# One tile in place of two for the decays of a state-space scan, with six buffers in place of four and two

## The chip, the cores and the metric

The kernel runs on one core of one Trainium2 chip. Its metric is the device time of one execution in microseconds (us), taken as the median of several runs. The core's engines are TensorE (PE, matrix products), VectorE (DVE), ScalarE (ACT), GpSimd (POOL) and SyncE (SP, which here issues nearly all DMA transfers). Each engine runs its own list of instructions strictly in order, and semaphores make one engine wait for another.

## The reference, cut to what matters

The program is one inference step of two layers, a gated pooling mixer and a gated Mamba-2 mixer (SSD), for 1024 prompt tokens and 64 sample tokens. The change touches the chunked scan of the second layer:

```python
a_cum_t = jnp.moveaxis(jnp.cumsum(a, axis=2), 2, -1)        # per chunk of 128 tokens, per head
causal = jnp.tril(jnp.ones((q, q), bool))
seg = a_cum_t[..., :, None] - a_cum_t[..., None, :]
L = jnp.exp(jnp.where(causal, seg, -jnp.inf))               # the decays
CB = jnp.einsum('bcign,bcjgn->bcgij', C, B)
W = CB[:, :, :, None] * L * dt_t[..., None, :]
y_diag = jnp.einsum('bcgeij,bcjgep->bcigep', W, x)
```

For each chunk of 128 tokens and each head a 128x128 matrix of decays L is formed, weighted with the products of C and B, and multiplied by the chunk's inputs.

## The kernel before

The tokens are worked in two halves, h=0 and h=1, of 512 prompt tokens and 32 sample tokens (544 columns). Activations lie with channels on the 128 partitions and tokens along the columns. The large projections (`product`, L172) split a weight tile of 128x1024 into a high and a low part (`whi`, `wlo`) and an activation likewise (`ah`, `al`); each 128x272 result takes 24 matmuls into one of three PSUM buffers called `big`, which an engine then copies or adds out: L184 into `u` on ACT, L761 and L762 into `z` on ACT and DVE, L790 and L791 into `X` on ACT and DVE. A PSUM buffer is free again only after this.

`stash` (L131 to L144) runs in the first half of the program, before about 650 us: it loads pieces of 128x512 of later weights, casts them (L141), subtracts (L142) and writes the low parts to DRAM, from where `wlo` is loaded later.

The scan (`ssd`, from L617) is called per half h, group g of heads and quad q of four heads, 16 calls in all, each with two pairs of chunks. For each chunk it loads the running sums of the decays, broadcast to all partitions (L632, a DMA on SP's queue, tile `bA`), masks them (L633, POOL), exponentiates them into a second tile `L` (L637, ACT, four instructions, one per head) and multiplies them by the chunk's weights `bs` (L638, DVE). For each pair of chunks PE then multiplies by the decays (L651, 16 matmuls into `dg`), reads the state (L665, `of` from `hf`) and forms the new states (L667, `stt`); POOL scales the old state (L672) and DVE adds the new one (L673). The sample tokens go the same way in `ssd_sample`: state tiles are loaded (L734), multiplied (L735), the new state is formed (L739), scaled on POOL (L741), added on DVE (L742) and stored (L743).

`ssd_common` (L598 to L603) makes, for a group, four transposes and four products on PE (L598, L599) and copies them to SBUF on ACT (L601 to `bs`, L603 to `bt`). At the end of a half, L858 (DVE) and L860 (POOL) scale the eight tiles `X` and add the residual.

The order of the instructions on each engine is not written by hand: the Tile framework's scheduler (L1028) decides it with its own model of time, from the program, the priorities (`tc.high_priority()` around PSUM copies and weight loads) and the number of buffers of each tile name. A tile name with `bufs=n` gives the n-th next tile the same memory, so that its first writer waits for the last reader of the tile n before it.

Of the kernel before, what the change touches and what calls it, by code (L numbers as in the profile page):

```python
# [9 lines left out]
F32 = mybir.dt.float32  # L10
F32R = mybir.dt.float32r
AF = mybir.ActivationFunctionType
ALU = mybir.AluOpType
# [3 lines left out]
P = 128  # L17
# [20 lines left out]
Q = 128  # L38
# [38 lines left out]
def pool_ssd_step(ctx, tc, xin, spool, sconv, sssm, w_pin, w_mix, w_pout, w_sin, w_dt, w_sout, params, consts,  # L77
                  y_out, pool_p, pool_s, conv_p, conv_s, ssm_p, ssm_s):
    nc = tc.nc
    V, S, G, PE = nc.vector, nc.scalar, nc.gpsimd, nc.tensor  # L80
# [4 lines left out]
    sp = ctx.enter_context(tc.tile_pool(name="sp", bufs=1))  # L85
# [45 lines left out]
    def stash(n):  # L131

        for k, src, a, b in todo[:n]:
            raw = sp.tile([P, 512], F32, name="L", bufs=4)[:, :b - a]
            load = nc.sync.dma_start(out=raw, in_=src[:, a:b])
            if behind[0] is not None:
                tc.add_manual_dep(load.ins, behind[0].ins.name,
                                  mybir.DependencyInfo(mybir.DependencyClass.NoSync, mybir.DependencyReason.DATA),
                                  reason="low parts come in behind the weights in use")
            hl = sp.tile([P, 512], F32R, name="bA", bufs=2)[:, :b - a]  # L140
            S.copy(hl, raw)  # L141
            V.tensor_tensor(out=hl, in0=raw, in1=hl, op=ALU.subtract)  # L142
            nc.sync.dma_start(out=low[k][:, a:b], in_=hl.bitcast(F32))
        del todo[:n]  # L144
# [139 lines left out]
    def project(src, act, u, evac):  # L284
        hi, lo = unit(src[u], k=LOW_IN + u if src is w_sin else None)
        stash(1)
        product(P, hi, lo, act, KT, P, 0, evac)
# [16 lines left out]
    def out_units(src, g, y, sink):  # L304
        for dpair in range(4):
            w = unit(src[g * 4 + dpair], k=LOW_OUT + g * 4 + dpair if src is w_sout else None)
            stash(1)
            out_unit(w, dpair, y, sink)


    def layer0(h, act, pending, nxt):
# [99 lines left out]
        def mix_part(g, p, z):  # L411
            tiles = []
            for mp in range(2):
                hi, lo = unit(w_mix[g * 2 + mp])
                stash(2 if h == 0 else 1)
                for tt in range(2):
                    t = mp * 2 + tt
                    y = z[t]

                    def gate(n, ps):  # L420
                        V.scalar_tensor_tensor(out=half(y, n), in0=ps, scalar=pcol(V_SC + g * 4 + t),
                                               in1=half(z[t], n), op0=ALU.mult, op1=ALU.mult)
                    product(P, hi, lo, p, 4, 256, tt * P, gate)
                    tiles.append(split(y, "y", t))
            return tiles
# [43 lines left out]
    acd = [dp.tile([NCH, NH, Q], F32, name=f"acd{h}") for h in range(2)]  # L469
# [137 lines left out]
    def heads(x):  # L607
        return x.rearrange("p (e d) -> p e d", e=4)
# [4 lines left out]
    def by_head(x, i):  # L613

        return x[:, i:i + 4, None].broadcast_to([x.shape[0], 4, HD])

    def ssd(h, g, q, x, ys, C, com, nat, cdb):  # L617
        h0 = g * 8 + q * 4
        hf = None
        if h == 1:  # L620
            hf = sp.tile([P, 2 * P], F32, name=f"hf{q}", bufs=2)
            nc.sync.dma_start(out=hf, in_=hsd[g, q])
        for c0 in range(0, NCH, 2):

            pd = sps.tile([P, 2, 2 * Q], F32, name="dg")
            xds, xss, Ls = [], [], []
            for c in (c0, c0 + 1):
                cs = slice(c * Q, (c + 1) * Q)
                ci = c * NH + h0

                bA = sp.tile([P, 4, Q], F32, name="bA", bufs=2)
                nc.sync.dma_start(out=bA, in_=acd[h][c:c + 1, h0:h0 + 4].broadcast_to([P, 4, Q]))  # L632
                G.affine_select(out=bA, in_=bA, pattern=[[0, 4], [1, Q]], compare_op=ALU.is_ge, fill=-1e30, base=0,  # L633
                                channel_multiplier=-1)
                L = sp.tile([P, 4, Q], F32, name="L", bufs=4)
                for e in range(4):
                    S.activation(out=L[:, e], in_=bA[:, e], func=AF.Exp, bias=nat[:, 0, ci + e:ci + e + 1])  # L637
                V.tensor_tensor(out=L, in0=L, in1=com[c][0].broadcast_to([P, 4, Q]), op=ALU.mult)  # L638
                px = sps.tile([P, 2 * P], F32, name="tr", bufs=2)
                for k in range(2):  # L640
                    PE.transpose(px[:, k * P:(k + 1) * P], x[:, k, cs], ident)  # L641
                xd = sp.tile([P, 2 * P], F32, name="xd", bufs=2)
                xs = sp.tile([P, 2 * P], F32, name="xs", bufs=2)
                for k, x1 in enumerate((xd, xs)):
                    V.tensor_tensor(out=heads(x1), in0=heads(px), in1=by_head(nat[:, 1 + k], ci), op=ALU.mult)
                xds.append(xd)
                xss.append(xs)
                Ls.append(L)
            for n in range(2):
                for e in range(4):  # L650
                    PE.matmul(pd[e % 2 * HD:(e % 2 + 1) * HD, e // 2, n * Q:(n + 1) * Q], xds[n][:, e * HD:(e + 1) * HD],  # L651
                              Ls[n][:, e], start=True, stop=True)
            first = 1 if hf is None else 0
            po = sps.tile([P, 2, 2 * Q], F32, name="of")
            bE = sp.tile([P, 2, 2 * Q], F32, name="bE")
            for n in range(2):
                c = c0 + n
                cs = slice(c * Q, (c + 1) * Q)
                ns = slice(n * Q, (n + 1) * Q)
                if hf is not None:  # L660
                    ev = ecd[h][c:c + 1, h0:h0 + 4].rearrange("c (k r) i -> c r k i", r=2)
                    for r in range(2):
                        nc.sync.dma_start(out=bE[r * 64:(r + 1) * 64, :, ns], in_=ev[:, r].broadcast_to([64, 2, Q]))
                    for k in range(2):
                        PE.matmul(po[:, k, ns], hf[:, k * P:(k + 1) * P], C[:, cs], start=True, stop=True)  # L665
                pst = sps.tile([P, 2 * P], F32, name="stt")
                PE.matmul(pst, com[c][1], xss[n], start=True, stop=True)  # L667
                hn = sp.tile([P, 2 * P], F32, name=f"hf{q}", bufs=2)
                if hf is None:
                    S.copy(hn, pst)  # L670
                else:
                    G.tensor_tensor(out=heads(hn), in0=heads(hf), in1=by_head(cdb, c * NH + h0), op=ALU.mult)  # L672
                    V.tensor_tensor(out=hn, in0=hn, in1=pst, op=ALU.add)  # L673
                hf = hn
            if first:
                S.copy(ys[:, :, c0 * Q:(c0 + 1) * Q], pd[:, :, :Q])
            fs = slice((c0 + first) * Q, (c0 + 2) * Q)
            V.tensor_tensor(out=ys[:, :, fs], in0=po[:, :, first * Q:], in1=bE[:, :, first * Q:], op=ALU.mult)
            V.tensor_tensor(out=ys[:, :, fs], in0=ys[:, :, fs], in1=pd[:, :, first * Q:], op=ALU.add)
        nc.sync.dma_start(out=ssm_p[g, q] if h == 1 else hsd[g, q], in_=hf)  # L680
# [99 lines left out]
    def layer1(h, act, started, pending, nxt):  # L780
# [26 lines left out]
        for g in range(NG):  # L807
# [6 lines left out]
            def quad(q):  # L814
                y = sp.tile([P, 2, T], F32, name="ys", bufs=2)
                ssd(h, g, q, xbc[2 * q], y, C, com, nat, cdb)
                ssd_sample(h, g, q, xbc[2 * q], y, C, scom, sat, cdb)
                return y
# [213 lines left out]
```

## Time and profile before

| what | value |
|---|---|
| runs (3), device time | 1584.18, 1584.54, 1586.19 us; median 1584.54 |
| the profiled execution | 1586.41 us, of which 1584.6 us are the profile's span |
| mean granted clock of TensorE in it | 0.995 of full speed |
| busy: PE, DVE, ACT, POOL | 98%, 68%, 46%, 21% of the span |
| chain of work that ended last | PE 87%, DMA 5%, DVE 4%, ACT 2% |
| share of L172's matmuls in that chain | 77% |

PE is busy nearly all of the time, so a change shows in the time where PE stands still or runs at a lower clock, and the other engines' idle time matters only where PE waits for them. The views used are the list of PE's waits, the views of one tile or line (its durations, first and last start, and what it waited for), the time line of one engine, the chain of waits, and tables of busy time by stretch.

### The profile page before, as it was taken

To read this page: it belongs to the slowest core of one execution; us is meant where nothing else is said; L and a number is where in the kernel's file an instruction comes from. 1 tells how busy PE (TensorE), PEld (TensorE's weight loads), DVE (VectorE), ACT (ScalarE), POOL (GpSimd) and SP (SyncE) were. 2 spreads that over 40 slices of the span, in tenths; PEclk is the share of its full clock that TensorE was granted. 3 is DMA by queue.
4 is the path that set the end of the run, shared out by engine and by line. 5 is a ranking of instruction groups with operands and counts; after the bars stand their busy time and mean duration, and the time that the engine had idled before them with its cause. 6 is when DMAs were issued, how large, how long until landed. Compare 5 with 4: busy or idle time off the path is not lost.

```text
span 1584.6 us, 33029 instructions
## 1 busy us (share of the span) xinstructions
PE 1554.3 (98%) x12644; PEld 1510.4 (95%) x12644; DVE 1085.3 (68%) x2068; ACT 734.0 (46%) x1454; POOL 333.9 (21%) x536
## 2 busy tenths in 40 slices
PE   9999999999999999999999999999998999999996
PEld 8999999999999999999999999999998999999995
DVE  7787778865557576658666476678778865755767
ACT  5553434544343434355565453543635645535432
POOL 1300000012100011013513112212326532231213
PEclk9999999999999999999999999999999999999998
DMA  7756656758555565565756656656666666565662
GB/s 258 245 191 186 206 167 218 252 183 274 185 172 188 168 195 187 165 197 154 244 183 200 201 173 218 209 190 219 206 206 210 215 217 205 176 218 176 210 218 86
DMA packets 163405, 315.80 MB, mean 199 GB/s; under 512 B 33072, under 2 KB 71600, under 8 KB 163248
## 3 DMA queue, kind: packets, MB, share of 16 engines
q1 hardware_dynamic: 163248, 313.70, 61.6%
q8 instruction: 99, 1.62, 0.4%
q14 instruction: 58, 0.48, 0.1%
HBM read 262.47 MB, written 51.16 MB: 198 GB/s over the span
## 4 chain that ended last, share of the span: by engine, by line
PE 87%; DMA 5%; DVE 4%; ACT 2%; issue 1%; POOL 1%; SPq 1%; DVEq 0%; POOLq 0%; ACTq 0%
PE big L172 77%; PE dg L651 2%; PE stt L667 2%; PE of L665 2%; DMA sq<-in_xin_dram 1%; PE tr L641 1%; DMA X<-in_xin_dram 1%; DVE X L858 1%; DMA L<-in_w_sin_dram 1%; PE stt L739 1%; PE big L392 1%; DMA out_ssm_s_dram<-ho 1%; PE of L735 1%; PE tr L599 0%; POOL ssq L251 0%
## 5 line engine op out<-in xcount | busy, mean ns | idle before, releaser
L172 PE MATMUL big<-ah,whi 128*128 128x272 f32 (+1 forms) x2304 | 668.5, 290 | 0.3 <-DVE X L428 0.3
L172 PE MATMUL big<-al,whi 128*128 128x272 f32 (+1 forms) x2304 | 668.6, 290 | 0.0
L172 PE MATMUL big<-ah,wlo 128*128 128x272 f32 (+1 forms) x2304 | 665.0, 289 | 0.0
L172 PEld LDWEIGHTS big<-ah,whi 128*128 128x128 f32 (+1 forms) x2304 | 432.7, 188 | 3.9 <-issue 2.3
L172 PEld LDWEIGHTS big<-ah,wlo 128*128 128x128 f32 (+1 forms) x2304 | 433.0, 188 | 2.8 <-issue 1.8
L172 PEld LDWEIGHTS big<-al,whi 128*128 128x128 f32 (+1 forms) x2304 | 432.8, 188 | 1.4 <-issue 0.4
L172 PE MATMUL big<-y,whi 128*128 128x272 f32 x2048 | 400.6, 292 | 4.7 <-DVE X L791 2.5
L155 ACT CAST whi<-raw 128x1024 fp32r<-128x1024 f32 (+1 forms) x228 | 237.6, 1042 | 334.2 <-PE big L172 248.2
L172 PEld LDWEIGHTS big<-y,whi 128*128 128x128 f32 x2048 | 322.9, 188 | 9.5 <-issue 3.1
L172 PE MATMUL big<-y,wlo 128*128 128x272 f32 x1024 | 298.3, 291 | 0.0
L157 DVE TENSOR_TENSOR wlo<-raw,whi 128x1024 fp32r<-128x1024 f32 x112 | 140.4, 1254 | 89.4 <-ACT whi L155 87.2
L172 PEld LDWEIGHTS big<-y,wlo 128*128 128x128 f32 x1024 | 193.5, 189 | 1.6 <-issue 1.0
L571 DVE SCALAR_TENSOR_TENSOR win<-u,par,win 128x556 f32<-128x556 f32 x144 | 119.4, 830 | 34.0 <-ACT win L569 31.6
L142 DVE TENSOR_TENSOR bA<-L,bA 128x512 fp32r<-128x512 f32 (+1 forms) x113 | 78.2, 693 | 31.3 <-ACT bA L141 27.9
L141 ACT CAST bA<-L 128x512 fp32r<-128x512 f32 (+1 forms) x113 | 69.9, 619 | 59.5 <-DMA L<-in_w_sin_dram 33.7
L172 PE MATMUL big<-p,whi 128*128 128x272 f32 x512 | 96.7, 288 | 0.0
L637 ACT ACTIVATE L<-bA,nat 128x128 f32<-128x128 f32 x256 | 80.2, 391 | 33.4 <-PE dg L651 24.8
L741 POOL TENSOR_TENSOR ho<-hs,cdb 128x256 f32<-128x256 f32 x64 | 47.2, 741 | 176.9 <-DMA out_ssm_s_dram<-ho 133.8
L172 PEld LDWEIGHTS big<-p,whi 128*128 128x128 f32 x512 | 80.3, 188 | 0.0
L331 POOL COPY uc<-u 128x15 f32<-128x15 f32 x30 | 22.2, 739 | 259.5 <-ACT u L184 169.2
L428 DVE TENSOR_TENSOR X<-X,big 128x272 f32<-128x272 f32 x128 | 54.3, 430 | 30.2 <-PE big L172 29.9
L184 ACT COPY u<-big 128x272 f32<-128x272 f32 (+2 forms) x192 | 52.5, 308 | 47.8 <-PE big L172 35.2
(212 smaller groups left out, 1964.7 us busy)
## 6 DMA issues: line engine op xcount, KB each, us to landing
wlo<-low SPq DMA_DIRECT2D x114, 512.0 KB, 3.9
raw<-in_w_sin_dram SPq DMA_DIRECT2D x80, 512.0 KB, 4.8
raw<-in_w_pin_dram SPq DMA_DIRECT2D x64, 512.0 KB, 3.9
low<-bA SPq DMA_DIRECT2D x112, 256.0 KB, 4.2
L<-in_w_sin_dram SPq DMA_DIRECT2D x80, 256.0 KB, 4.3
raw<-in_w_sout_dram SPq DMA_DIRECT2D x34, 512.0 KB, 4.7
raw<-in_w_pout_dram SPq DMA_DIRECT2D x32, 512.0 KB, 3.8
bA<-acd SPq DMA_DIRECT2D x64, 256.0 KB, 3.9
```

The source lines that it names most:

```text
L141: S.copy(hl, raw)
L142: V.tensor_tensor(out=hl, in0=raw, in1=hl, op=ALU.subtract)
L155: S.copy(hi[:, :cols], raw[:, :cols])
L157: V.tensor_tensor(out=lo[:, :cols], in0=raw[:, :cols], in1=hi[:, :cols], op=ALU.subtract)
L172: PE.matmul(ps, w[:, wsl], x[:, cols], start=first, stop=kt == kts - 1 and a == 2)
L184: S.copy(out, ps)
L428: return lambda n, ps: V.tensor_tensor(out=half(X[d], n), in0=half(X[d], n), in1=ps, op=ALU.add)
L571: V.scalar_tensor_tensor(out=a[:, :n], in0=x[:, k:k + n], scalar=pcol(V_CW + ti * 4 + k), in1=a[:, :n], op0=ALU.mult, op1=ALU.add)
L637: S.activation(out=L[:, e], in_=bA[:, e], func=AF.Exp, bias=nat[:, 0, ci + e:ci + e + 1])
L651: PE.matmul(pd[e % 2 * HD:(e % 2 + 1) * HD, e // 2, n * Q:(n + 1) * Q], xds[n][:, e * HD:(e + 1) * HD], Ls[n][:, e], start=True, stop=True)
L665: PE.matmul(po[:, k, ns], hf[:, k * P:(k + 1) * P], C[:, cs], start=True, stop=True)
L741: G.tensor_tensor(out=heads(ho), in0=heads(hs), in1=by_head(cdb, (NCH + b) * NH + h0), op=ALU.mult)
```

## The change

`bA` as a tile name of its own disappears. In `ssd` the decays are loaded into a tile `L`, masked in it and exponentiated in it, in place; `L` has six buffers where `L` had four and `bA` two, so that the memory taken is the same (2 KB a partition each). In `stash` the tile `hl` moves from `bA` to `L`. Each engine issues as many instructions as before. In the changed file every line from L636 on has a number lower by one.

```diff
     def stash(n):
...
-            raw = sp.tile([P, 512], F32, name="L", bufs=4)[:, :b - a]
+            raw = sp.tile([P, 512], F32, name="L", bufs=6)[:, :b - a]
...
-            hl = sp.tile([P, 512], F32R, name="bA", bufs=2)[:, :b - a]
+            hl = sp.tile([P, 512], F32R, name="L", bufs=6)[:, :b - a]
...
     def ssd(h, g, q, x, ys, C, com, nat, cdb):
...
-                bA = sp.tile([P, 4, Q], F32, name="bA", bufs=2)
-                nc.sync.dma_start(out=bA, in_=acd[h][c:c + 1, h0:h0 + 4].broadcast_to([P, 4, Q]))
-                G.affine_select(out=bA, in_=bA, pattern=[[0, 4], [1, Q]], compare_op=ALU.is_ge, fill=-1e30, base=0,
+                L = sp.tile([P, 4, Q], F32, name="L", bufs=6)
+                nc.sync.dma_start(out=L, in_=acd[h][c:c + 1, h0:h0 + 4].broadcast_to([P, 4, Q]))
+                G.affine_select(out=L, in_=L, pattern=[[0, 4], [1, Q]], compare_op=ALU.is_ge, fill=-1e30, base=0,
                                 channel_multiplier=-1)
-                L = sp.tile([P, 4, Q], F32, name="L", bufs=4)
                 for e in range(4):
-                    S.activation(out=L[:, e], in_=bA[:, e], func=AF.Exp, bias=nat[:, 0, ci + e:ci + e + 1])
+                    S.activation(out=L[:, e], in_=L[:, e], func=AF.Exp, bias=nat[:, 0, ci + e:ci + e + 1])
```

The scheduler places the work of the scan anew. Three places of the program follow, one of them on two engines; the numbers behind the names are the tiles.

SP at the opening of the scan (h=0, around 700 us before), from the loads of the first chunk pair on. First the order before:

```order
L632 DMA bA_8874<-acd0_143 128x512
L543 DMA esd0_151<-d2_8502 32x32
L663 DMA bE_8901<-ecd0_145 64x2x128 x2
L705 DMA bAs_8986<-asd0_149 32x128
L159 DMA wlo_9137<-low19_105 128x1024
L752 DMA bEs_9053<-esd0_151 64x2x32
L152 DMA raw_9469<-in_w_sin_dram 128x1024
L752 DMA bEs_9053<-esd0_151 64x2x32
L632 DMA bA_8919<-acd0_143 128x512
L632 DMA bA_8937<-acd0_143 128x512
```

And the order of the change in the same place:

```order
L632 DMA L_8873<-acd0_143 128x512
L543 DMA esd0_151<-d2_8502 32x32
L662 DMA bE_8899<-ecd0_145 64x2x128 x2
L632 DMA L_8917<-acd0_143 128x512
L159 DMA wlo_9133<-low19_105 128x1024
L632 DMA L_8934<-acd0_143 128x512
L152 DMA raw_9461<-in_w_sin_dram 128x1024
L704 DMA bAs_8982<-asd0_149 32x128
L751 DMA bEs_9049<-esd0_151 64x2x32 x2
L632 DMA L_9201<-acd0_143 128x512
```

The loads of the second pair (`bA_8919` and `bA_8937`, now `L_8917` and `L_8934`) have moved up past two weight loads and three loads for the samples; the third pair's follow where the second's were.

ACT in the same place, before:

```order
L569 ACTIVATE win0_8729<-u_8665,par_76 128x556
L184 COPY u_8738<-big_8747 128x272
L709 ACTIVATE bAs_8986<-bAs_8986 32x128
L155 CAST whi_9410<-raw_9408 128x1024
L184 COPY u_8738<-big_8773 128x240
L184 COPY u_8738<-big_8773 128x4x8
L637 ACTIVATE L_8924<-bA_8919,nat_8495 128x128 x3
L601 COPY bs_8813<-tr_8810 128x128
L603 COPY bt_8815<-tr_8810 128x128
L637 ACTIVATE L_8924<-bA_8919,nat_8495 128x128
L601 COPY bs_8820<-tr_8817 128x128
L603 COPY bt_8822<-tr_8817 128x128
```

And in the change:

```order
L569 ACTIVATE win0_8729<-u_8665,par_76 128x556
L636 ACTIVATE L_8917<-L_8917,nat_8495 128x128 x4
L184 COPY u_8738<-big_8747 128x272
L636 ACTIVATE L_8934<-L_8934,nat_8495 128x128 x4
L155 CAST whi_9402<-raw_9400 128x1024
L184 COPY u_8738<-big_8773 128x240
L184 COPY u_8738<-big_8773 128x4x8
L601 COPY bs_8813<-tr_8810 128x128
L603 COPY bt_8815<-tr_8810 128x128
L601 COPY bs_8820<-tr_8817 128x128
L603 COPY bt_8822<-tr_8817 128x128
```

The second pair's eight exponentials have moved ahead of three PSUM copies and a weight cast, and no exponential stands directly ahead of or between the copies L601 and L603 any more.

DVE at the end of the first half (around 1202 us before), where the eight L858 stand; before:

```order
L679 TENSOR_TENSOR ys<-ys,dg 128x2x256
L235 COPY rr<-tr 128x272 x2
L858 TENSOR_TENSOR X_10997<-X_10997,rr 128x544
...
L858 TENSOR_TENSOR X_11218<-X_11218,rr 128x544
L742 TENSOR_TENSOR ho<-ho,stt 128x256
L762 SCALAR_TENSOR_TENSOR z_15808<-z_15808,big 128x272
L754 TENSOR_TENSOR ys<-of,bEs 128x2x32
```

And in the change:

```order
L678 TENSOR_TENSOR ys<-ys,dg 128x2x256
L235 COPY rr<-tr 128x272
...
L741 TENSOR_TENSOR ho<-ho,stt 128x256
L857 TENSOR_TENSOR X_10981<-X_10981,rr 128x544
...
L857 TENSOR_TENSOR X_11202<-X_11202,rr 128x544
L753 TENSOR_TENSOR ys<-of,bEs 128x2x32
L761 SCALAR_TENSOR_TENSOR z_15768<-z_15768,big 128x272
```

The addition L742 of the first sample state (L741 in the changed file) has moved ahead of the eight scalings; the evacuation L762 of a `big` buffer (now L761) still stands behind them.

ACT in the first group of the second half (around 1293 us before), where copies L790 stand behind exponentials; before:

```order
L790 COPY X3_17066<-big_17067 128x272
L802 ACTIVATE sq_17225<-p2_16144 128x544
L637 ACTIVATE L_17720<-bA_17715,nat_14370 128x128 x4
L709 ACTIVATE bAs_16773<-bAs_16773 32x128
L637 ACTIVATE L_17738<-bA_17733,nat_14370 128x128 x4
L802 ACTIVATE sq_17233<-p2_16144 128x544
L155 CAST whi_17242<-raw_17240 128x1024
L790 COPY X3_17066<-big_17081 128x272
```

And in the change:

```order
L801 ACTIVATE sq_17177<-p2_16104 128x544
L801 ACTIVATE sq_17185<-p2_16104 128x544
L789 COPY X3_17018<-big_17019 128x272
L155 CAST whi_17194<-raw_17192 128x1024
L789 COPY X3_17018<-big_17033 128x272
L636 ACTIVATE L_17732<-L_17732,nat_14338 128x128 x4
L789 COPY X4_17053<-big_17054 128x272
L636 ACTIVATE L_17749<-L_17749,nat_14338 128x128 x4
```

The second copy of `X3` stood behind eight exponentials, two squares and a cast; now only the cast stands between the two copies of `X3`, and the exponentials follow them.

## Rows read from the trace of the kernel before

**Rows 1.** The page, part 1: busy time of each engine

```profile
PE 1554.3 (98%) x12644; PEld 1510.4 (95%) x12644; DVE 1085.3 (68%) x2068; ACT 734.0 (46%) x1454; POOL 333.9 (21%) x536
```

**Rows 2.** PE's waits: instruction <- its releaser: us in total, times, longest

```profile
PE stt L739 <- DVE ho L742: 4.1, 1, 4.1
...
PE tr L598 <- ACT bt L603: 1.9, 1, 1.9
...
PE of L665 <- DVE hf L673: 1.2, 1, 1.2
PE big L172 <- ACT X L790: 1.0, 1, 1.0
```

**Rows 3.** Tile `L`: ns min/median/max, first and last start us

```profile
L651 PE MATMUL dg<-L,xd x512: 272/273/324, 726.8 to 1516.5; 128*64 128x128 f32 x171
...
L638 DVE TENSOR_TENSOR L<-L,bs x64: 670/684/1168, 710.9 to 1486.1; 128x512 f32<-128x512 f32 x64
```

**Rows 4.** Tile `bA`: one line's durations, idle time by releaser, landing

```profile
L633 POOL TENSOR_SCALAR_AFFINE_SELECT bA<-bA x64: 627/635/1631, 698.8 to 1478.8; 128x512 f32<-128x512 f32 x64
...
  DMA bA<-acd: 114.8, 51
...
  PE dg L651: 24.8, 14
...
DMA to landing us min/median/max: 2.0/4.1/7.3
```

**Rows 5.** Time line of SP: start us, us, instruction

```profile
697.29 1.32 SPq L663 DMA_DIRECT2D bE<-ecd  x2
...
702.81 1.01 SPq L632 DMA_DIRECT2D bA<-acd  x2
...
728.87 1.76 SPq L632 DMA_DIRECT2D bA<-acd  x2
```

**Rows 6.** Chain of waits, 702 to 712 us

```profile
702.81 6.10 DMA bA<-acd
```

**Rows 7.** Time line of ACT, 700 to 711 us; [idle before <- releaser]

```profile
704.82 0.44 ACT L184 COPY u<-big 128x240 f32<-128x240 f32 x2
709.72 0.99 ACT L637 ACTIVATE L<-bA,nat 128x128 f32<-128x128 f32 x3 [4.46 <-POOL bA L633]
```

**Rows 8.** Busy time by stretch: us, PE (x), PEld, DVE, ACT, POOL, PEclk, DMA

```profile
700.00:711.00 11.00, 9.14 (x74) 8.92 (x72) 3.17 (x8) 6.29 (x23) 1.36 (x7) 1.00 0.65 225
...
712.00:714.00 2.00, 2.00 (x12) 2.00 (x11) 0.98 (x3) 2.00 (x5) 0.71 (x2) 0.51 0.45 165
714.00:716.00 2.00, 2.00 (x12) 2.00 (x12) 2.00 (x4) 1.06 (x7) 0.91 (x1) 0.63 0.72 155
```

**Rows 9.** Time line of DVE, 1202 to 1214 us

```profile
1202.10 11.36 DVE L858 TENSOR_TENSOR X<-X,rr 128x544 f32<-128x544 f32 x8
...
1213.71 0.43 DVE L762 SCALAR_TENSOR_TENSOR z<-z,big 128x272 f32<-128x272 f32 x1
```

**Rows 10.** Line L858: ns min/median/max

```profile
L858 DVE TENSOR_TENSOR X<-X,rr x8: 717/1848/1887, 1202.1 to 1211.6; 128x544 f32<-128x544 f32 x8
```

**Rows 11.** Time line of POOL, 1207 to 1215 us

```profile
1207.49 7.17 POOL L860 TENSOR_TENSOR X<-X,sq 128x544 f32<-128x544 f32 x4
```

**Rows 12.** Busy time by stretch, two later places

```profile
1214.00:1217.00 3.00, 3.00 (x13) 2.94 (x14) 2.96 (x10) 1.14 (x3) 1.97 (x3) 0.50 0.50 142
...
1410.00:1413.00 3.00, 3.00 (x33) 2.83 (x30) 1.87 (x6) 2.45 (x9) 0.61 (x1) 1.00 0.67 216
```

**Rows 13.** Time line of ACT, 1295 to 1299 us

```profile
1295.63 1.26 ACT L637 ACTIVATE L<-bA,nat 128x128 f32<-128x128 f32 x4
...
1297.35 1.03 ACT L155 CAST whi<-raw 128x1024 fp32r<-128x1024 f32 x1
1298.29 0.92 ACT L790 COPY X<-big 128x272 f32<-128x272 f32 x3
```

**Rows 14.** Time line of POOL, 1404 to 1408 us

```profile
1406.89 0.61 POOL L741 TENSOR_TENSOR ho<-hs,cdb 128x256 f32<-128x256 f32 x1 [2.49 <-DMA out_ssm_s_dram<-ho]
```

## The prediction

> **What bounds the kernel now.** I read the page first: PE is busy 98% of the span [rows 1], so the time is PE's work plus the little that PE loses. The change issues the same matmuls, so it can move only what PE loses, by standing still or by running at a low clock. The next view is therefore the list of PE's waits. It holds 14 lines, the longest 4.1 us and 1.9 us [rows 2], and the reader is to see what is not in it: no wait of PE on the tile `L` or on L651, the matmuls that read the decays. The view of the tile says why. The first L638, which finishes a tile of decays, starts at 710.9 us and the first L651 at 726.8 us; the last ones at 1486.1 and 1516.5 [rows 3]. The decays are there long before PE wants them. The third view is that of what waits for buffers: POOL stood 114.8 us, in 51 waits, for the loads of the decays, and ACT 24.8 us, in 14, for L651 to release an `L` [rows 4]. This is what the change attacks, and neither engine is the bound, so this idle time is worth nothing by itself. What counts are the places where another instruction, for which PE does wait, stands behind this work in its engine's queue. I name four of them: A, the opening of the scan (wait on L603); B, the end of the first half (wait on L742); C, in the second half (wait on L790); D, later in it (wait on L673) [rows 2].
>
> The Trainium skill bears on this: "Perfetto Trace Analysis", section Optimization Strategy, says that the same gap repeating on the engine that should be saturated can mean that there is no memory for the next tile, and names buffer counts. Here the repeating gaps are on POOL and ACT and none is on PE, so by that rule two more buffers give nothing: 1584.5 us, which is my first rival.
>
> **A, the opening of the scan.** PE waits 1.9 us for a copy L603 on ACT [rows 2]. The copy stands in ACT's queue behind three exponentials, which had waited 4.46 us for POOL [rows 7], POOL for the second chunk pair's load. That load was issued at 702.81 and took 6.10 us [rows 6]. It could not go earlier, since `bA` has two buffers and the exponentials of the first pair had to be done. With six buffers it goes right behind the loads of `bE`, which end at 697.29 + 1.32 = 698.6 [rows 5]: 4.2 us earlier, more than the 1.9 us of the wait. After the stop PE also ran slowly. From 700 to 711 us it did 74 matmuls in 9.14 busy us, 0.123 us each; from 712 to 716 it did 24 in 4.0 us, where 24 x 0.123 = 2.95 us would do, with a granted clock of 0.51 and 0.63, that is near 1.2 GHz in place of 2.4 [rows 8]. So A costs 1.9 + 1.05 = 3.0 us now. What eats into it: the loads of a chunk land in 2.0 to 7.3 us [rows 4], and ACT now has all eight exponentials of the second pair, 8 x 0.32 = 2.5 us (four took 1.26 us) [rows 13], and then a cast of about 1.03 us [rows 13] ahead of the copies, which had been done by 704.82 + 0.44, before the wait [rows 7]. If the fourth tile's load, one issue later, takes 7.3 us, all of the 4.2 us is used up by these 3.5 us and the issue, and A stays as it is: 0. If it takes 4.1 us, all goes: -3.0. I take -2.0, nearer to the median landing.
>
> **B, the end of the first half.** PE waits 4.1 us for L742, which stands behind eight L858 that take 11.36 us on DVE [rows 2, 9]. In the change L742 stands ahead of them, so the named wait goes. But L762, which empties a `big` buffer, still stands behind them. In both orders PE can run three such buffers, 3 x 24 = 72 matmuls, from the start of that projection on, and counted in the order of before, exactly these 72 stand between that start and the L739 at which PE stopped. L762 itself started only at 1213.71, when PE's wait was ending [rows 9]. What is late next is therefore the matmul on the unreleased buffer, at nearly the same time: later by L742 and L754 ahead of it (0.4 and 0.2 us), earlier by what else DVE has shed in front. I take +0.5, with -0.5 to +1.0. Clock included, B costs 4.1 us and 3.0 - 13 x 0.123 = 1.4 us now [rows 12] and keeps that. The eight L858 would have to become shorter: one took 0.72 us, the median 1.85 us [rows 10], while POOL's L860 ran beside them at 7.17 / 4 = 1.79 us each [rows 11]. The change leaves both in the same place.
>
> The Trainium skill, "SBUF — State Buffer", section Who interferes with whom, says that a DVE instruction with two SBUF inputs contends with a GpSimd one that reads SBUF. By that rule an L860 delayed past the L858 would end these after 8 x 0.72 = 5.7 us and save B's 5.5 us; the order gives no such delay.
>
> **C.** PE waits 1.0 us [rows 2] for a copy L790 at 1298.29, behind a cast, a square and eight exponentials, four of which began at 1295.63 and took 1.26 us [rows 13]. In the change these stand behind the copy. 1.26 us is more than 1.0, so the wait goes: -1.0. The cost appears on the next copies: each of two stands behind four exponentials. A `big` buffer of this projection takes 12 matmuls, 1.5 us; two buffers beside the one in work cover 3.0 us, and four exponentials and a copy take 1.26 + 0.31 = 1.6 us. They are covered as long as no exponential waits for its tile longer than about 1.4 us. Bounds -1.0 to +1.0.
>
> **D.** PE waits 1.2 us for L673 [rows 2]. That sum waits for POOL's L672, which stands behind L741, and this one waits 2.49 us for the store of an older sample state [rows 14]. The change does not touch the chain, but the scheduler puts about four matmuls fewer between the states and their use, 4 x 0.123 = 0.5 us less cover. I take +0.5. Bounds: -1.2, if the store lands sooner, to +3.0, since a stop of 1.2 us leaves the clock at 1.00 [rows 12] while the one of 1.9 us at A was followed by 0.51, so that a slightly longer stop here could cost the 1.05 us of A as well.
>
> **The rest.** Masking and exponentials cost what they did, 0.635 us [rows 4] and 0.32 us; writing in place adds no instruction. The part of `stash` stands in the same order before 650 us, so 0. The load L632 now waits on SP for the L651 of three pairs earlier, and weight loads stand behind it. The wait is not new in size: SP issued such a pair at 728.87 [rows 5] already, behind the first L651 at 726.8. Between 726.8 and 1516.5 there are 32 groups of L651, one each 25 us [rows 3], and the chain load, mask, exponentials, product (4.1 + 0.6 + 1.3 + 0.7 = 6.7 us) fits many times. I take 0, with 0 to +3.
>
> **Sum.** -2.0 + 0.5 - 1.0 + 0.5 = -2.0 us. The profiled execution took 1586.41 us (span 1584.6 and 1.8 around it), so it becomes 1584.4. The median of the runs is 1584.54, 1.9 us below the profiled one, and becomes 1582.5.
>
> **Rivals.** First, nothing: the decays were never what PE waits for [rows 2, 3], A's loads land late, and one stop gives way to the next. Speaks for it that POOL's and ACT's waits are off the path; against it that A and C hang on exponentials in ACT's queue. 1584.5 us.
>
> Second, slower: exponentials now stand earlier in ACT's queue, in front of copies that empty `big`, and when one waits for its load and mask, the copies wait with it. It decides from where such a wait exceeds the 3.0 us of cover in a projection of 12 matmuls a buffer. The wait at A was 4.46 us [rows 7], which would be a stop of 1.5 us, with a clock loss as at A 2.5 us each. One in place of the gains gives 1587.0, two 1589.5; I put it at 1588.5. Speaks for it that all exponentials of the scan have moved forward in the order; against it that six buffers let the loads go earlier as well.
>
> Third, a larger gain: A in full, C, and D's 1.2, with B as it is: -5.2 us, 1579.3. For it speaks the median landing of 4.1 us [rows 4]; against it that D's chain is a store and the sample states, not decays.
>
> **How the numbers follow.** Forecast 1582.5, chance 0.46, its own range 1580.0 to 1584.5. Nothing 0.18, slower 0.22, larger gain 0.14. The bound of what a measurement can tell here is 0.2%, 3.2 us: below 1581.4 or above 1587.7. Faster: the larger gain and about 0.4 of the forecast's case, 0.14 + 0.18 = 0.32. Slower: most of the second rival and a little from unknown stops, 0.18 + 0.02 = 0.20. Same: 0.48. The range goes to 1577.8, below the larger gain, and to 1588.8, beyond the slower one's middle.
>
> **What would show it.** In the list of PE's waits after: A right if the wait on L603 is under 1 us and the clock stays at 1.00 behind it; wrong if it is still near 1.9. B right if the wait on L742 is gone and one of near 4 us on L762 stands in its place; wrong if both are gone. C right if the 1.0 us on L790 is gone and no other on L790 over 0.5 us has come. D shows as the wait on L673, 1 to 2 us expected. The forecast is wrong as a whole if a stop of over 2 us stands at a place that has none now, above all a matmul of `big` waiting for ACT while ACT waits for POOL, or if weight loads come late behind L632 on SP.

## The result, and the profile after

The changed kernel takes 1610.34 us (median of 4 runs, 1608.46 to 1613.83) where the kernel before takes 1585.27 us (median of 4): a ratio of 1.0149, with a 95% interval of 1.0131 to 1.0167, some 24 us slower. The profiled execution took 1608.46 us, its span is 1606.5 us, 21.9 us above that of before. The forecast was 1582.5 us, its range 1577.8 to 1588.8.

PE did as many matmuls as before (the page, part 1, to be read beside [rows 1]):

```profile
PE 1562.7 (97%) x12644; PEld 1515.5 (94%) x12644; DVE 1068.4 (67%) x2068; ACT 734.2 (46%) x1454; POOL 351.6 (22%) x536
```

The instructions are as many as before, so the time went into what PE loses. Its list of waits after the change, eight of its lines (us in total, times, longest), answers to [rows 2]:

```profile
PE big L172 <- DVE X L790: 5.3, 4, 2.2
PE of L664 <- ACT hf L669: 5.1, 2, 3.6
PE stt L738 <- DVE ho L741: 5.0, 4, 1.3
PE of L747 <- ACT yn L744: 3.3, 4, 1.4
PE big L172 <- ACT X L789: 2.8, 3, 2.2
PE tr L205 <- POOL ssq L251: 2.6, 1, 2.6
PE tr L598 <- ACT bt L603: 1.0, 1, 1.0
...
PE of L664 <- DVE hf L672: 0.8, 2, 0.4
```

Again none is on the decays themselves. The whole list adds up to 30.6 us, that of before to 17.4: 13.2 us of the 21.9. PE was also busy 8.4 us longer with as many matmuls (1562.7 us against 1554.3), while its mean granted clock went from 0.995 to 0.992 of full speed; what is left, 0.3 us, are gaps too short for the list. The loss is spread over the scan; its first 300 us show how much. Busy time by stretch (the count behind PE is the one to read), after the change and then before it:

```profile
700.00:1000.00 300.00, 289.72 (x2350) 275.65 (x2350) 181.76 (x395) 151.66 (x355) 89.07 (x146) 0.98 0.59 188
```

```profile
700.00:1000.00 300.00, 298.07 (x2463) 286.19 (x2462) 193.77 (x410) 157.87 (x366) 89.10 (x155) 0.99 0.62 199
```

113 matmuls fewer in the same 300 us are 14 us, as an estimate at 0.123 us each.

The engine that changed its behaviour is ACT. The first line is its largest new wait in the list of ACT's waits after (us, times, longest); the second answers to it before, from the view of the tile `bA` (us, times):

```profile
ACT L L636 <- POOL L L633: 101.1, 39, 8.9
```

```profile
  POOL bA L633: 6.8, 3
```

Before the change the exponentials waited 6.8 us for masked tiles, after it 101.1 us. Subtracting the ends of the masks from the starts of the first exponential of each tile in the two traces (tiles 7 to 64) gives a median of 7.5 us before and 0.03 us after: before, the masked tile lay ready for long; now the exponential usually stands at the head of ACT's queue until the mask is done. The largest stop of PE shows what that does. Time lines of SP, POOL, ACT and PE around 966 to 980 us after the change:

```profile
966.06 0.38 SPq L632 DMA_DIRECT2D L<-acd  x1
...
967.44 0.42 SPq L632 DMA_DIRECT2D L<-acd  x1
...
971.27 0.63 POOL L633 TENSOR_SCALAR_AFFINE_SELECT L<-L 128x512 f32<-128x512 f32 x1 [4.37 <-DMA L<-acd]
...
975.29 0.63 POOL L633 TENSOR_SCALAR_AFFINE_SELECT L<-L 128x512 f32<-128x512 f32 x1 [2.05 <-DMA L<-acd]
...
971.94 1.28 ACT L636 ACTIVATE L<-L,nat 128x128 f32<-128x128 f32 x4 [6.69 <-POOL L L633]
975.96 0.40 ACT L636 ACTIVATE L<-L,nat 128x128 f32<-128x128 f32 x1 [2.74 <-POOL L L633]
976.26 1.03 ACT L155 CAST whi<-raw 128x1024 fp32r<-128x1024 f32 x1
977.20 0.98 ACT L636 ACTIVATE L<-L,nat 128x128 f32<-128x128 f32 x3
978.09 0.35 ACT L669 COPY hf<-stt 128x256 f32<-128x256 f32 x1
...
978.49 1.22 PE L664 MATMUL of<-p,hf 128*128 128x128 f32 x4 [3.61 <-ACT hf L669]
```

Two loads are issued at 966.06 and 967.44 and land about 5 and 8 us later; ACT, which has come to these eight exponentials at 965.2, stands 6.69 and 2.74 us; the copy L669 of a state into `hf`, for which PE does wait, stands behind them. The matmuls that read these decays run at 1056 us, some 80 us later. Behind the stop the granted clock is 0.50:

```profile
979.00:982.00 3.00, 3.00 (x14) 2.82 (x13) 1.75 (x5) 0.00 (x0) 0.74 (x2) 0.50 0.43 168
```

Other stops of this kind, behind an exponential that waited 4 to 6 us, are at 763.7 (1.5 us, L669), 863.6 (2.2, L789), 1302.6 (0.8, L744) and 1439.7 (1.4, L744). One at 782.8 (0.9, L744) stands behind eight exponentials too, but only 1.03 us of waiting for a mask is in front of it, and two loads of ACT's function tables, 1.28 us each, as well. The second half also has the same pattern on DVE: at 1412 us PE waits 2.2 us for L790, which stands behind the sample mask L706, and this behind its load:

```profile
1409.89 0.97 DVE L706 TENSOR_SCALAR bAs<-bAs,sat 32x32 f32<-32x32 f32 x4 [4.21 <-DMA bAs<-asd]
```

The end of the first half, place B, went otherwise than forecast in this execution. Time lines of DVE and POOL after, to be read beside [rows 9, 11], and the view of the line L859 (ns min/median/max):

```profile
1216.03 5.17 DVE L857 TENSOR_TENSOR X<-X,rr 128x544 f32<-128x544 f32 x8
...
1216.83 8.23 POOL L859 TENSOR_TENSOR X<-X,sq 128x544 f32<-128x544 f32 x3 [1.97 <-DVE X L857]
...
L859 POOL TENSOR_TENSOR X<-X,sq x8: 1343/1571/5590, 1216.8 to 1235.8; 128x544 f32<-128x544 f32 x8
```

The eight scalings take 5.17 us in place of 11.36, and no stop of PE stands beside them. PE's n-th matmul, which is 13.2 us later than before at 1210 us of the kernel before, is 8.5 us later at 1220. At 1240 it is 14.1 us later again, with stops of 1.05 and 1.35 us for L741 at 1225 and 1231 and of 2.6 us for POOL's L251 at 1249.

### The profile page after: what moved, and what is told of

It reads as the page before. It is cut to its first block, busy times and chain, and to the rows that moved or that the text cites. A ratio compares the mean times of both kernels' runs of the same rounds, so it can differ in the third digit from the quotient of the medians.

```text
span 1606.5 us, 33010 instructions
## 1 busy us (share of the span) xinstructions
PE 1562.7 (97%) x12644; PEld 1515.5 (94%) x12644; DVE 1068.4 (67%) x2068; ACT 734.2 (46%) x1454; POOL 351.6 (22%) x536
## 5 line engine op out<-in xcount | busy, mean ns | idle before, releaser
L172 PE MATMUL big<-y,whi 128*128 128x272 f32 x2048 | 406.3, 294 | 8.3 <-DVE X L790 5.3
L172 PEld LDWEIGHTS big<-y,whi 128*128 128x128 f32 x2048 | 326.6, 190 | 13.9 <-DVE X L790 6.6
L636 ACT ACTIVATE L<-L,nat 128x128 f32<-128x128 f32 x256 | 81.4, 390 | 101.3 <-POOL L L633 101.1
L141 ACT CAST L<-L 128x512 fp32r<-128x512 f32 (+1 forms) x113 | 69.9, 619 | 67.9 <-DMA L<-in_w_sin_dram 51.8
L142 DVE TENSOR_TENSOR L<-L 128x512 fp32r<-128x512 f32 (+1 forms) x113 | 78.7, 697 | 30.0 <-ACT L L141 29.7
L740 POOL TENSOR_TENSOR ho<-hs,cdb 128x256 f32<-128x256 f32 x64 | 57.7, 907 | 162.1 <-DMA out_ssm_s_dram<-ho 108.9
L331 POOL COPY uc<-u 128x15 f32<-128x15 f32 x30 | 26.8, 892 | 258.0 <-ACT u L184 167.9
L172 PE MATMUL big<-p,wlo 128*128 128x272 f32 x256 | 73.6, 288 | 0.0
```

Source lines behind the costliest of these rows:

```text
L172: PE.matmul(ps, w[:, wsl], x[:, cols], start=first, stop=kt == kts - 1 and a == 2)
L331: G.tensor_copy(out=uc[:, m], in_=u[:, LP:LP + HALO])
L636: S.activation(out=L[:, e], in_=L[:, e], func=AF.Exp, bias=nat[:, 0, ci + e:ci + e + 1])
L740: G.tensor_tensor(out=heads(ho), in0=heads(hs), in1=by_head(cdb, (NCH + b) * NH + h0), op=ALU.mult)
```

## The experiments

Ratios are to the kernel before on the same chip; the kernel before takes 1586 to 1589 us there. Theory O: the tiles cost nothing, the new order of the instructions costs everything. It became theory H: the exponentials stand on ACT ahead of their data. In the experiments with a held order (e1, e2, e5, e8 to e12, e14), each instruction gets an edge (order only, no wait) from the one before it in a list, engine by engine. The code is shortened here, as it is for e2, e5 and e7 to e13:

```diff
+    for each engine: for (last, k) in the engine's list:
+        tc.add_manual_dep(traced[k], traced[last].name, NoSync)
```

**e1: the changed tiles in the order of before.**

> The changed tiles (one L with six buffers, in place), with every engine's instructions held in the order of the kernel before. Theory O (the new order costs the 25 us, the tiles themselves nothing): 1582 to 1587 us, and the waits of PE as before (about 4.1 us on L742, 1.9 us on L603). Theory M (a tile used in place is freed only by L651, so that loads on SP are held up and with them the weights): 1595 us or more, with new waits of PE on whi, wlo or L.

Measured: 0.9972 (0.9954 to 0.9989). PE's waits are those of before:

```profile
PE stt L738 <- DVE ho L741: 4.2, 1, 4.2
...
PE tr L598 <- ACT bt L603: 2.5, 2, 1.8
```

Theory M falls. The tiles themselves cost nothing; in the old order they are even 0.3% ahead of the kernel before, the most of all versions here (e8 is 0.1% ahead). Where that 0.3% comes from was not looked into.

**e2: ACT alone in the order of before, the rest scheduled freely.**

```diff
-    for each engine:
+    for ACT alone:
```

> The change, with ACT's instructions alone held in the order of the kernel before; the other engines as the scheduler places them. Theory O in its narrow form (exponentials placed early on ACT wait for POOL and hold up the PSUM copies behind them): most of the loss goes, 1585 to 1593 us, and ACT's 101 us of waiting for the masked tiles fall below 40. Rival (the loss comes from the late loads on SP, or from DVE and POOL): 1600 us or more.

Measured: 1.0037 (1.0017 to 1.0057). The 1595.51 us are above the range expected, but the kernel before took 1589.40 us on this chip. The idle time of ACT for masked tiles (view of the tile `L`) is gone:

```profile
  POOL L L633: 1.3, 2
```

About 18 of the 24 us go with ACT's order (1.0149 - 1.0037 = 0.0112), though the free engines were placed anew around it, so this is no clean share.

**e3: the stash's part of the change alone.**

```diff
-            hl = sp.tile([P, 512], F32R, name="bA", bufs=2)[:, :b - a]
+            hl = sp.tile([P, 512], F32R, name="L", bufs=4)[:, :b - a]
```

> The kernel before with hl of the stash moved to L (four buffers), the scan with its two tiles as before. The changed kernel was 2.4 us ahead at 412 us. If the stash's part gives that: 1581 to 1583 us, with the waits of PE around 372 to 395 us gone. If that gain came from six buffers and not from the shared name: 1584 to 1587 us. Any theory that puts the loss into the stash: 1595 us or more.

Measured: 0.9993 (0.9974 to 1.0012). No effect. The 2.4 us by which the changed kernel was ahead at 412 us do not come with its order either: e5, which has the changed kernel's own order there, stood 1.1 us behind the kernel before at that point.

**e4: the scan in place, with four buffers, the stash as before.**

```diff
-                bA = sp.tile([P, 4, Q], F32, name="bA", bufs=2)
+                L = sp.tile([P, 4, Q], F32, name="L", bufs=4)
```

> The stash as before (raw in L with four buffers, hl in bA with two); the scan loads, masks and exponentiates in place in L, with four buffers. Theory O: the scheduler places the exponentials early here too, so 1595 to 1612 us. Theory S (six buffers let the loads and exponentials run too far ahead; with four they stay near their use): 1583 to 1590 us.

Measured: 1.0093 (1.0059 to 1.0127), 1604.24 us. Theory O as expected: the number six is not needed for a loss. It is smaller here, 15 us in place of 24 (what the rest is of, two buffers more or the stash, was not tried). ACT's wait is there again:

```profile
ACT L L636 <- POOL L L633: 103.8, 45, 6.3
```

**e5: the change's own order, exponentials four places later on ACT, the product after them twelve later on DVE.**

```diff
 the change's order, on ACT, for each tile:
-    L636 x4, a, b, c, d
+    a, b, c, d, L636 x4
 on DVE: L637 behind the twelve instructions that followed it
```

> The changed kernel with all its engines held in its own order, except that on ACT the four exponentials of each tile stand four instructions later, and on DVE the product L637 that follows them twelve instructions later. Theory H (the exponentials stand on ACT where the load after the release of L has not landed yet, and hold up the copies behind them): ACT's 101 us of waiting for POOL's masked tiles fall below 50, and the time falls by 8 to 18 us against the change, to a ratio of 1.004 to 1.010. Rival D (the sample state, DVE and SP orders cost the time): within 4 us of the change, ratio 1.012 to 1.018.

Measured: 1.0108 (1.0090 to 1.0126), just above the range of H. ACT's wait fell from 101 to 1.1 us, but there are other waits on DVE (PE's list, then DVE's time line):

```profile
PE dg L650 <- DVE xd L644: 5.6, 7, 2.6
...
PE big L172 <- DVE z L761: 3.7, 1, 3.7
...
1210.30 11.37 DVE L857 TENSOR_TENSOR X<-X,rr 128x544 f32<-128x544 f32 x8
...
1221.73 0.42 DVE L761 SCALAR_TENSOR_TENSOR z<-z,big 128x272 f32<-128x272 f32 x1
```

The first came with the products moved on DVE. The second did not: it is the wait at place B as the prediction had it, an L761 behind eight scalings that here take 11.37 us, in the order that the change has at this place.

Compare when PE starts its n-th matmul: from matmul 5,500 to 8,000 (695 to 1001 us before) the change loses 14.1 us against the kernel before, e5 only 3.3. After that the change loses 10.1 more and e5 12.4. These are single executions. In e1, e3, e8, e12 and e13, which lose next to nothing, the first figure is -3.5 to -0.8 and the second 0.3 to 5.5, so a difference of a few us in them says nothing.

**e6: two tiles for a chunk again, both from one pool of six.**

```diff
+                bA = sp.tile([P, 4, Q], F32, name="L", bufs=6)
...
+                L = sp.tile([P, 4, Q], F32, name="L", bufs=6)
```

> One name L with six buffers for stash and scan, as in the change, but the scan takes two of them for a chunk again: it loads and masks into one and exponentiates into another. Theory H: the load needs no release by L651 any more, only the exponentials do, so that its landing is hidden; ACT waits under 30 us for masked tiles, and the ratio is 0.995 to 1.005. Rival S (any new order of the scan costs about 1%): ratio 1.008 or more.

Measured: 1.0155 (1.0134 to 1.0176). My expectation was wrong: working in place is not what matters. The list of ACT's waits:

```profile
ACT L L637 <- POOL L L633: 103.5, 40, 4.8
```

The exponentials here begin 0.03 us after the mask (median), so they too had nothing left that held them back longer than the load does. Their release comes too early for that: none begins before the L651 of the tile five before it has ended, 42 of 60 begin before that of the tile four before has, and the L651 of the tile five before ends 4.7 us (median) ahead of the mask.

**e7: loads and masks at high priority.**

```diff
+                with tc.high_priority():
+                    nc.sync.dma_start(out=L, ...)
+                    G.affine_select(out=L, in_=L, ...)
```

> The change with the loads L632 and the masks L633 at high priority. Theory H: most loads stand at the release of their buffer already (40 of 58 within 0.5 us of the end of the L651 that frees it), so ACT's wait for masked tiles stays above 60 us and the ratio at 1.008 to 1.02. Rival L (the loads are late because they stand behind sample loads on SP): ACT's wait falls below 40 us and the ratio below 1.006.

Measured: 1.0245 (1.0225 to 1.0265), worse than H's range. Rival L falls, since ACT's wait stays. PE has further waits that the change has not, 9.2 us in three for POOL's L546 and 5.2 us in one for L762; they were not looked into.

```profile
ACT L L637 <- POOL L L634: 105.0, 41, 8.9
```

**e8 and e12: the end of the first half, in the order of before.** Both move evacuations on DVE in among the scalings; e12 goes further and moves one L740 on POOL ahead of three L859.

```diff
 DVE, order of before:
-    L857 x8, L741, L761, L753, L706 x4, L761
+    L857, L741, L857 x2, L761, L857 x3, L761, L857 x2, L753, L706 x4            (e8)
+    L857, L741, L857 x2, L761, L857 x2, L761, L741, L857 x3, L753, L706 x4      (e12)
```

> The changed tiles with every engine in the order of the kernel before, except at the end of the first half on DVE: of the eight scalings L857 the first stands ahead of L741, two more ahead of the first L761, three more ahead of the second L761, the last two behind it. The stop of 4.2 us at L738 and the low clock behind it (5.5 us together) should go or shrink below 1.5 us, so 3 to 6 us less than with the order of before alone: ratio 0.992 to 0.996. Rival: another wait takes its place (L761's own buffer, or the residual stream late at the next projection), ratio as without it, 0.997.

> The changed tiles in the order of the kernel before, with the end of the first half altered on DVE as the time before (which left a stop of 4.3 us for the second L741) and further: this second L741 stands right behind the second L761, after the fifth L857, and on POOL the L740 of the third state stands three instructions earlier. The stop and its low clock (about 5.5 us) go: ratio 0.992 to 0.996, and no wait of PE over 2 us is left between 1190 and 1220 us. Rival (the chain moves on to the third state or to L794): ratio 0.997 to 0.999.

Measured: 0.9986 (0.9976 to 0.9996) and 1.0002 (0.9990 to 1.0014). Neither gains on e1. The stop only moved, first to the next state's sum, then to the one after (PE's waits in e8, then in e12, at 1213 and 1224 us):

```profile
PE stt L738 <- DVE ho L741: 4.3, 1, 4.3
```

```profile
PE stt L738 <- DVE ho L741: 6.3, 1, 6.3
```

The rivals were right in that another wait takes its place; both ratios are a little above theirs.

**e9: the suspected cost alone, added to the good order.** As e1, with only the exponentials moved forward on ACT.

```diff
 the order of before, on ACT, for each tile from the seventh on (by 1 to 77 places, median 4.5):
-    a, b, c, d, L636 x4
+    L636 x4, a, b, c, d
```

> The changed tiles with every engine in the order of the kernel before (ratio 0.997), but on ACT the exponentials of each tile from the seventh on moved forward, to where ACT stood 1.5 us after the load was issued or, if later, where POOL began the instruction ahead of the mask. Nothing else moves. Theory H (exponentials that stand on ACT ahead of their data hold up the copies behind them): ACT waits 70 to 140 us for masked tiles and the ratio rises by 0.005 to 0.013, to 1.002 to 1.010. Rival D (ACT has room for these waits, the loss comes from the orders of DVE, POOL and PE): ratio below 1.001.

Measured: 1.0282 (1.0261 to 1.0302), 45 us above the kernel before. The sign is that of H, the size more than twice the largest that I expected. The change itself has these 58 exponentials forward by about as much (0 to 76 places, median 4, against the same order), but with the other engines placed to go with it. View of the tile `L` (ACT's idle time) and PE's waits:

```profile
  POOL L L633: 146.2, 41
```

```profile
PE big L172 <- ACT X L789: 8.8, 3, 6.2
PE stt L738 <- DVE ho L741: 7.3, 3, 5.5
PE tr L598 <- ACT bt L603: 6.3, 3, 4.0
```

This shows that exponentials placed early on ACT are enough to cause a loss of this kind; its size is not that of the change. Rival D falls.

**e10 and e11: SP's order exchanged.**

```diff
-    PE, DVE, ACT, POOL, SP in one kernel's order
+    PE, DVE, ACT, POOL as in the change, SP as before     (e10)
+    PE, DVE, ACT, POOL as before, SP as in the change     (e11)
```

> The changed kernel with PE, DVE, ACT and POOL held in its own order and SP in the order of the kernel before. Theory H: the loads cannot come before the release of their buffer, so 1.010 to 1.018, as the change. Rival L (loads stand too late on SP, behind sample loads and stores): ratio below 1.007.

> The changed tiles with SP in the order of the changed kernel, PE, DVE, ACT and POOL in the order of the kernel before. Theory H: exponentials stand late enough on ACT, so a later load costs nothing: 0.995 to 1.002. Rival L: 1.005 or more.

Measured: 1.0392 (1.0374 to 1.0410) and 1.0270 (1.0251 to 1.0288). Either way it is slower than both kernels, so the two say nothing on where the change's loss comes from: exchanging SP's order alone costs more than the effect sought. Both miss H's ranges; rival L's is met in e11 and not in e10. In e11 the largest wait has nothing to do with decays:

```profile
PE stt L738 <- DVE ho L741: 18.5, 8, 5.2
```

**e13: the change, scheduled freely, with the gate put back.**

```diff
+                    if len(read) >= 2:      # the last L651 of each chunk pair so far
+                        tc.add_manual_dep(decay.ins, read[-2].ins.name, Sync)
```

> The change, scheduled freely, with one more wait: the exponentials of a tile wait on ACT for the L651 of two chunk pairs before, as they did when L had four buffers; the loads keep their six. Theory H (the release of L by L651 had held the exponentials back until load and mask were long done; the change took this gate away, the scheduler put them right behind the load, and ACT stands still until it lands): with the gate back ACT waits under 30 us for masked tiles, and the ratio is 0.994 to 1.003. Rival R (any new order of the scan costs about 1%, gate or not): 1.007 or more.

Measured: 1.0009 (0.9995 to 1.0024), 1587.88 us. The loss is gone, with all engines scheduled freely, and the range of H is met. View of the tile `L`, what ACT's idle time ended with (L657 is the matmul of the decays here, L635 the mask):

```profile
  PE dg L657: 39.6, 15
...
  POOL L L635: 6.4, 5
```

This is the picture of [rows 4]: ACT waits for PE, not for a load. Rival R falls.

**e14: as e5, three places on ACT and six on DVE, from the seventh tile on.**

> The changed kernel with all engines held in its own order, but from the seventh tile on the four exponentials of a tile stand three instructions later on ACT and the product L637 six later on DVE (four and twelve the time before, which took away ACT's wait and brought new waits of PE on DVE of some 12 us). Theory H: ACT's wait for masked tiles under 40 us, fewer of the new waits, ratio 1.003 to 1.009. Rival D: 1.011 or more.

Measured: 1.0152 (1.0124 to 1.0180), no gain over the change: H's expectation failed. ACT's wait for masked tiles fell to 4.2 us, and in the first stretch (matmuls 5,500 to 8,000) e14 loses 1.8 us where the change loses 14.1; behind it, it loses 15.4 where the change loses 10.1, with stops of 2.1, 1.5, 2.4, 3.7 and 2.4 us at instructions of DVE. That of 3.7 us is again the L761 behind eight scalings in 11.37 us. What share of the change's loss in its second half is ACT's is left open by e5 and e14. In the change itself the stops behind a waiting exponential add up to 2.2 us there (0.8 and 1.4).

## Why the prediction was wrong

The step that failed is "The rest", where I put the load's new wait and the exponentials at 0, with 0 to +3. In the two profiled executions it was some 26 us, what came of C and D included: of the 21.9 us between them, 2.3 had been gained before the scan and 2.5 at A, and 0.9 were lost at B. I asked whether the chain load, mask, exponentials and product fits between two groups of L651, and it does: PE never waits for decays, before or after. I did not ask what ACT does while this chain runs.

In the kernel before, two waits held an exponential: its mask, and the release of an `L` by L651 [rows 4]. The release, the end of the L651 of four tiles before, came 6.7 us (median) after the mask's end, and the exponentials began 7.5 us after it. So the release set where they stood; the 24.8 us of waiting for L651, which I called worth nothing, were what kept the load's latency away from ACT. The change moved the release ahead of the load. What is left between release and exponential is the load and the mask. The load takes this long from issue to landing (view of the line L632 after, 64 loads):

```profile
DMA to landing us min/median/max: 3.1/5.1/7.7
```

The scheduler placed the exponentials so close behind that ACT stands for a part of it in 39 of 64 tiles. They then end 76 us (median) before the first matmul that reads them, where it was 31 us. e13 shows that putting this one wait back undoes the loss, e9 that placing the exponentials early makes one, e1 that the tiles do nothing by themselves. Open is how much of the loss behind 1000 us comes through ACT and how much through the orders that the scheduler made around it on DVE.

Point by point:

- The second rival had the mechanism, exponentials earlier on ACT with PSUM copies behind them, and the right sign, and my sign of being wrong as a whole came: at 863.6 a matmul of `big` waits 2.2 us for ACT, which had waited for POOL. The rival's size was wrong. I priced one or two stops of 1.5 us, from a wait of 4.46 us less 3.0 us of cover. There were six stops of 0.8 to 3.6 us behind ACT, the waits of the exponentials reached 8.9 us, and the copies were also L669 and L744, whose results PE reads itself. I held against it that six buffers let loads go earlier: they did only for the first six tiles. From the seventh on a load waits for a release, and 35 of 58 are issued within 0.5 us of the end of the freeing L651.
- A was right in size: the wait on L603 fell from 1.9 to 1.0 us (I had written under 1) and the clock stayed at 1.00 behind it; PE's matmuls gained 2.5 us there, where I had -2.0.
- B did not come as forecast in the profiled execution of the change. I forecast that L762 would take the place of L742 and add 0.5 us. Neither wait of 4 us is there, since the scalings took 0.72 us each; "the change leaves both in the same place" did not hold there. In all, B lost 0.9 us by 1240 us, near +0.5 by luck. In e5 and e14, with the change's order at this place, the scalings took 1.85 us (median) and PE waits 3.7 us for L761, as I had it.
- C was right at its place (0.3 us is left there), but the same wait came at another: 2.2 us for L789 at 863.6, behind an exponential that waited 4.06 us, where I had put the limit at 1.4.
- D: the forecast was 1 to 2 us; the longest wait on L672 is 0.4.
- The landing of 2.0 to 7.3 us, median 4.1, that I used is that of all transfers of the tile `bA`, those of the stash too; the 64 loads of the decays took 3.0 to 7.3, median 3.9.
- The rival "nothing" was wrong too: PE had no gaps on the decays, and the time still moved, because the buffers changed the order. The rule of the Trainium skill that I set beside it ("Perfetto Trace Analysis", Optimization Strategy: repeating gaps on the saturated engine can mean too few buffers) says nothing against adding them where there are none; that conclusion was mine.

## What to carry to other kernels

As here, a wait of an engine off the path can be what keeps an in-order queue in a good order. Before a buffer is added or merged, look at each instruction that waited for its release, ask what its next releaser is, and, if that is a DMA, what stands behind the instruction in its engine's queue. Where a scheduler places the work, a change of buffers is a change of order: holding the old order with the new tiles (e1) separates the two in one run, and one added wait for each tile (e13) brought the time back.

## What the runs showed of the hardware

The same eight DVE instructions of 128x544 took 1.85 us each (median) with POOL's instructions of this size beside them at 1.79 us [rows 10, 11], and 0.72 us each in the changed kernel. There the first of POOL's took 5.59 us and ended 1.2 us after the last of DVE's, and the two behind it took 1.37 and 1.35 us with DVE past its eight. In one case both were slowed, in turn, in the other POOL alone, for as long as DVE ran its eight. The Trainium skill, "SBUF — State Buffer", Who interferes with whom, says that a DVE instruction with two SBUF inputs contends with a GpSimd one that reads SBUF, and that issue order decides who blocks. That they contend fits. The order of the starts does not tell the two cases apart: POOL's first began 0.17 us behind the start of DVE's second in the kernel before and 0.16 us in the changed one. In e5 and e14, which have the change's order here, it began at 0.15 and 0.16 us, and the two engines took turns as in the kernel before. What decided is open.
